# Moving two-input sums and low parts from GpSimd to VectorE in a layer's output mixer and first feed-forward stage, and splitting one weight unit into a spare place

## The chip, the cores and the metric

One Trainium2 chip; the program runs on one of its cores. The engines are TensorE (PE in the profile, with its weight loads as PEld), VectorE (DVE), ScalarE (ACT), GpSimd (POOL) and SyncE (SP, which only issues transfers). The metric is the device time of one execution in microseconds (us): for the kernel before, the median of three runs is 722.89 us (722.44 to 723.54).

## What is computed

One layer of a streaming encoder on a sequence of 512 rows and 1024 columns, all in float32:

```python
u = rms_norm(h, g_mix)
z = u @ w_in                                    # q, k, v of two attentions, two gates
y_a = sliding_window_attention(...) @ w_br_swa
y_b = forgetting_attention(...) @ w_br_fox
mixed = gates[:, :, 0] * y_a + gates[:, :, 1] * y_b
h = h + mixed @ w_mix_out
u = rms_norm(h, g_mlp)
h = h + jnp.square(jax.nn.relu(u @ w_ff1)) @ w_ff2
ple_gate = jax.nn.sigmoid(rms_norm(h, g_ple) @ w_ple_gate)
h = h + ple_gate * (p @ w_ple_proj)             # p: 512 x 256
return rms_norm(h, g_final)
```

## The kernel before

**High and low parts.** Every float32 operand of a matrix product is split into a high part (a rounded copy, made by a cast on ACT, line 332) and a low part (the value minus its high part, a subtraction on two inputs in SBUF, line 334). PE multiplies high by high, high by low and low by high (lines 77 to 79, 918 and 1302). So a block of weights can be used only after its load has landed, ACT has cast it and another engine has subtracted.

**Seven products instead of eight.** The large products (input gates, mixer, both feed-forward stages) are cut into two by two blocks and computed with seven block products, numbered 1 to 7. Their weight operands are quadrants of the weights or sums of quadrants, their other operands are quadrants or sums of quadrants of the activations, and the results are added and subtracted into place. Operand numbers 1, 2 and 3 use a quadrant of the weights as it is; numbers 4 to 7 need a sum. `sum_source` (from line 275) makes that sum in place: by an accumulating transfer from the POOL queue (line 306), by an addition on POOL (line 302: only numbers 6 and 7 of the second column half of the first feed-forward stage) or by an addition on DVE (line 304: numbers 5 and 7 of the second feed-forward stage).

**Units.** The program walks through a list of weight units, of 128x1024 elements in the stages spoken of here. `emit_split(i)` writes the high and low part of unit i into buffers `u<i>h` and `u<i>l`, of which there are four each, used in turn. `advance(i)` splits all units up to i; it is called ahead of each product with the unit that is wanted some steps later, and that distance is what the text calls the look-ahead. After each unit it also issues loads for later units as far as a place for them is free. The names `wq`, `wq_t`, `wq_c` and `wq_gb` are places of raw weights; `emit_dma` (line 271) loads into them from SP. SP runs through its loads in program order, so one that waits for its place holds up all behind it.

**The mixer** (`h + mixed @ w_mix_out`) runs in the order `MIX_STEPS`, "A1 A2 B1 A5 B2 B5 A6 B6 A3 B3 A7 B7 p0 A4 B4 p4": A and B are column halves of the output, the digit is the operand number, and p0 and p4 stand for the product with `w_ple_proj`. Its units are u43 (A1), u44 (A2), u45 (B1), u46 (A5), u47 (B2), u48 (B5), u49 (A6), u50 (B6), u51 (A3), u52 (B3), u53 (A7), u54 (B7), u55 (p0; its halves lie in `at_ff`), u56 (A4), u57 (B4) and u58 (p4, in `at_ff` too). Its other operand is `mixed`, held as `r_a` (upper rows) and `r_b` (lower rows). `branches` adds the two gated attention outputs into them (line 1024 on POOL for `r_a`, line 1030 on DVE for `r_b`), `mix_sum` (line 1064, on POOL) forms the sums of quadrants, and `mix_ops` splits the results into high and low parts, most of the second set into the tile `u_mix`. That tile has 8240 elements a partition; behind a shift of 48 the six operands take 6144, and the last 2048 lie unused. `rows_out` adds each product into the residual `h_sb` (lines 1124 and 1126).

**The first feed-forward stage** comes next: units u59 on, with u62 (b2), u63 (a5), u64 (b5), u65 (a6), u66 (b6) and u67 (a7) ahead of the first units of the second stage, `s2`, which are mixed in from u71 on. Between mixer and stage lies a norm: `norm_scale` gives `n_xn` (line 378), PE transposes it (line 1194), and `t2_top`, `t2_sums`, `t2_sums2`, `t2_sum4` and `t2_rest` form the operands of the stage (lines 1215 to 1245), with their sums `s3` and `s4` on POOL (lines 1235 and 1245). `win_out` adds the products up (line 933), `ff1_lo` and `ff1_act` apply the squared ReLU and split it (line 1430).

**What sets the order.** In the mixer and the first steps of the feed-forward stage the order of ACT's and DVE's instructions is the written one; each engine runs its list in that order, and an instruction that waits holds up all behind it. Low parts listed in `POOL_LO` (units u44, u51 to u54 and u58) are subtracted on POOL, all others on DVE. The places of the raw feed-forward weights are dealt out ahead by a small planner: each block gets the place that comes free first. One of these places, "t2", is planned as free from the unit of ("f1", 1, 2) on, u62, since the tile `p_sb` (the input `p`) lies there before.

Of the kernel before, what the change touches and what calls it, by code (L numbers as in the profile page):

```python
# [8 lines left out]
F32 = mybir.dt.float32  # L9
F32R = mybir.dt.float32r  # L10
AF = mybir.ActivationFunctionType
ALU = mybir.AluOpType
# [35 lines left out]
MIX_STEPS = "A1 A2 B1 A5 B2 B5 A6 B6 A3 B3 A7 B7 p0 A4 B4 p4"  # L48
POOL_LO = [("mx", g, pn) for g, pn in ((0, 2), (0, 3), (1, 3), (0, 7), (1, 7))] + [("pp", 1)]
ET = mybir.EngineType  # L50
# [3 lines left out]
def layer_kernel(ctx: ExitStack, tc: tile.TileContext, x, p, g_mix, w_in, b_forget, swa_sinks,  # L54
# [154 lines left out]
    for n, r in enumerate(used):  # L209
        if first_ff <= r < last_ff:  # L210
            if not free_at:
                for w2 in (True, False):
                    for z, m in enumerate(ring[w2][-2:]):
                        for y in range(2):
                            free_at[w2, z, y] = last_use[used[m]]
                late_places = unit_of["f1", 1, 2]
                free_at.update({"t2": late_places, "c6": late_places,
                                "c7": late_places, "gb": late_places})
# [63 lines left out]
    def sum_source(i):  # L282
# [13 lines left out]
        if pn in (1, 2, 3):  # L296
            q = quadrant(i, pn in (2, 3), pn == 3)
        else:
            q = quadrant(i, 0, pn == 7)
            other = quadrant(i, *{5: (0, 1), 7: (1, 1), 6: (1, 1), 4: (1, 0)}[pn])  # L300
            if key in (("f1", 1, 6), ("f1", 1, 7)):
                nc.gpsimd.tensor_tensor(q, q, other, ALU.add)
            elif key[0] == "s2" and pn in (5, 7):
                nc.vector.tensor_tensor(q, q, other, ALU.add)
            else:
                nc.gpsimd.dma_start(q, other, accum_op=ALU.add)  # L306
        sources[i] = q if key[0] != "f1" and key[0] != "g" else q.rearrange("q k (j c) -> q k j c", c=P)

    def emit_split(i):
# [19 lines left out]
        for a in range(np_):  # L329
            n = shape[1] // np_  # L330
            z = slice(a * n, a * n + n)
            nc.scalar.copy(hi[:, z], src[:, z])  # L332
            on_pool = order[i][0] in POOL_LO
            (nc.gpsimd if on_pool else nc.vector).tensor_tensor(lo[:, z], src[:, z], hi[:, z].bitcast(F32), ALU.subtract)  # L334
        order[i][2] = (hi, lo)
# [667 lines left out]
    def branches(m):  # L1003
# [45 lines left out]
    def mix_place(g, pn):  # L1049
        n = {(0, 1): 0, (0, 2): 1, (0, 4): 4, (0, 5): 2, (0, 6): 3, (0, 7): 6, (0, 3): 7,  # L1050
             (1, 4): 5}.get((g, pn))
        if n is not None:
            return at2.tile([P, 2, 2, 256], F32R, tag=f"d{n}", name=f"mo{g}_{pn}")
        if "u" not in r_whole:
            r_whole["u"] = up.tile([P, 2 * KT * S + SHIFT], F32R, tag="u", bufs=1, name="u_mix")
        n = (1, 2, 5, 6, 3, 7).index(pn) * 1024 + SHIFT
        return r_whole["u"][:, n:n + 1024].rearrange("q (z k s) -> q z k s", z=2, k=2)

    def mix_sum(g, n):
# [3 lines left out]
                       (r11, r22, r11, ALU.add), (r12, r11, r12, ALU.subtract))[n]  # L1063
        nc.gpsimd.tensor_tensor(o, a, b, op)

    look["split"] = 0
    done = None
    for t in P2_STEPS:
# [18 lines left out]
        if t[0] == "br":  # L1087
# [3 lines left out]
            if t[1] == 4:  # L1091
                mix_ops(0, (5, 7, 6, 3))
            if t[1] == 5:
                mix_ops(1, (1,))
# [133 lines left out]
    def t2_sums(tb):  # L1228
# [5 lines left out]
            lambda: nc.vector.tensor_tensor(s1, trs[tb, 1], a21, ALU.subtract))  # L1234
        nc.gpsimd.tensor_tensor(s3, a_raw[0][t2_cols(tb)], a21, ALU.subtract)

# [5 lines left out]

    def t2_sum4(tb):
        a21, s1, s2, s3, s4 = sums[tb]
        nc.gpsimd.tensor_tensor(s4, a_raw[1][t2_cols(tb)], s2, ALU.add)

# [12 lines left out]
    def p_transposed():  # L1259
        pth, ptl = pT[:] = [spare(4 + i, f"pT_{'hl'[i]}", (P, 2, S)) for i in range(2)]  # L1260
        for k in range(2):
            tr = psA.tile([P, 4, P], F32, tag="tr", bufs=3, name=f"p_tr{k}")
            for tb in range(NT):
                nc.tensor.transpose(tr[:, tb, :], p_sb[:, tb, k * P:(k + 1) * P], ident)
            hi_lo(pth[:, k, :].rearrange("q (t c) -> q t c", c=P),
# [57 lines left out]
    for t in MIX_STEPS.split():  # L1323
        if t == "B5":
# [144 lines left out]
    t2_sum4(2)  # L1469
    pp_put(5, pp_mm(5))  # L1470
    advance(f1_0 + 2)
    t2_sums2(3)
    pp_put(6, pp_mm(6))
    pp_put(7, pp_mm(7))
    t2_rest(5)
    advance(f1_0 + 3)
    done, late, later = None, None, {}
    for n, st_ in enumerate(steps):
# [148 lines left out]
```

## Time and profile before

| | |
|---|---|
| median of three runs | 722.89 us (722.44 to 723.54) |
| the profiled execution | 722.85 us |
| its span | 721.1 us |
| mean granted PE clock | 0.995 of full speed |
| PE busy | 702.6 us, 97% of the span |
| DVE busy | 552.3 us, 77% |
| ACT busy | 457.0 us, 63% |
| POOL busy | 130.4 us, 18% |

The mixer's second half and the norm behind it lie at about 311 to 362 us of the span, the first feed-forward stage up to the first product of the second stage at about 362 to 410 us. In the profile a group "engine line op out<-in" is one kind of instruction; "x" counts instructions, and a bracket at the end of a timeline's row names the idle time ahead of an instruction and what ended it. "PEclk" is the share of full speed at which PE was allowed to run.

### The profile page before, as it was taken

To read this page: it belongs to the slowest core of one execution; us is meant where nothing else is said; L and a number is where in the kernel's file an instruction comes from. 1 tells how busy PE (TensorE), PEld (TensorE's weight loads), DVE (VectorE), ACT (ScalarE), POOL (GpSimd) and SP (SyncE) were. 2 spreads that over 40 slices of the span, in tenths; PEclk is the share of its full clock that TensorE was granted. 3 is DMA by queue.
4 is the path that set the end of the run, shared out by engine and by line. 5 is a ranking of instruction groups with operands and counts; after the bars stand their busy time and mean duration, and the time that the engine had idled before them with its cause. 6 is when DMAs were issued, how large, how long until landed. Compare 5 with 4: busy or idle time off the path is not lost.

```text
span 721.1 us, 11513 instructions
## 1 busy us (share of the span) xinstructions
PE 702.6 (97%) x4205; PEld 623.7 (86%) x4205; DVE 552.3 (77%) x918; ACT 457.0 (63%) x851; POOL 130.4 (18%) x152
## 2 busy tenths in 40 slices
PE   8999999999999999989979999999999999999996
PEld 7988888888888998867879889988999889988885
DVE  6557887877696667756897995799669975998555
ACT  6547888779862553345677745875478547875452
POOL 1011211100004501563450102000200011010001
PEclk9999999999999999999999999999999999999998
DMA  9166446660363896498668499947895699268103
GB/s 296 60 171 149 131 111 165 152 178 1 118 205 87 165 331 206 78 225 266 174 156 256 84 270 175 247 115 173 227 241 145 136 259 210 73 142 304 50 2 116
DMA packets 75272, 119.88 MB, mean 166 GB/s; under 512 B 6856, under 2 KB 44752, under 8 KB 75216
## 3 DMA queue, kind: packets, MB, share of 16 engines
q1 hardware_dynamic: 66000, 86.25, 38.1%
q0 software_dynamic: 8928, 32.51, 24.4%
q8 instruction: 33, 0.54, 0.3%
q10 hardware_dynamic: 288, 0.39, 0.2%
q14 instruction: 23, 0.19, 0.1%
HBM read 72.93 MB, written 4.19 MB: 107 GB/s over the span
## 4 chain that ended last, share of the span: by engine, by line
PE 86%; DVE 5%; issue 3%; ACT 3%; DMA 1%; POOL 1%; POOLq 0%; DVEq 0%; ACTq 0%
PE pf L77 5%; PE pf L79 5%; PE pf L78 5%; PE (3, 's2')x L1302 3%; PE (0, 's2')x L1302 3%; PE (2, 's2')x L1302 3%; PE (1, 's2')x L1302 3%; PE h_sc L769 2%; PE h_pv L839 2%; PE h_tr L827 2%; PE psy L77 2%; PE psy L78 2%; PE psy L79 2%; PE vb L483 2%; PE va L483 2%
## 5 line engine op out<-in xcount | busy, mean ns | idle before, releaser
L306 POOL DMA_DIRECT2D wq<-wq x35 | 30.5, 933 | 160.8 <-DVE u43l L334 26.0
L787 ACT ACTIVATE s<-s,h_nm 128x128 f32<-128x128 f32 (+1 forms) x64 | 32.6, 512 | 5.9 <-DVE h_nm L780 5.1
L74 DVE TENSOR_TENSOR h_ptl<-h_tr,h_pth 128x512 fp32r<-128x512 f32 (+2 forms) x40 | 22.9, 604 | 3.9 <-ACT h_pth L73 3.6
L1024 POOL TENSOR_TENSOR r_a<-gl,gl 128x512 f32<-128x512 f32 x4 | 6.1, 1526 | 83.8 <-ACT u25h L332 75.8
L73 ACT CAST h_pth<-h_tr 128x512 fp32r<-128x512 f32 (+2 forms) x40 | 19.5, 523 | 1.8 <-PE h_tr L827 1.4
L368 POOL TENSOR_SCALAR n_ms<-acc 128x1 f32<-128x1 f32 x15 | 4.9, 329 | 83.7 <-ACT sgp L1534 38.9
L483 PE MATMUL va<-wv_h,u 128*128 128x320 f32 x64 | 19.9, 317 | 0.0
L827 PE MATMUL h_tr<-ident,s 128*128 128x128 f32 x136 | 19.6, 277 | 0.2 <-ACT s L807 0.2
L483 PE MATMUL vb<-wv_h,u 128*128 128x328 f32 x64 | 19.6, 313 | 0.0
L1529 DVE TENSOR_TENSOR sgp<-sgp,pp 128x512 f32<-128x512 f32 (+1 forms) x9 | 5.7, 633 | 15.8 <-ACT sgp L1528 15.8
L839 PE MATMUL h_pv<-h_pth,v 128*128 128x256 f32 (+1 forms) x64 | 17.3, 291 | 0.0
L839 PE MATMUL h_pv<-h_ptl,v 128*128 128x256 f32 (+1 forms) x64 | 16.9, 305 | 0.3 <-DVE h_ptl L74 0.3
L1134 ACT ACTIVATE junk<-h_sb 128x512 f32<-128x512 f32 x16 | 10.0, 624 | 11.3 <-DVE h_sb L1124 4.9
L827 PEld LDWEIGHTS h_tr<-ident,s 128*128 128x128 f32 x136 | 15.1, 141 | 2.0 <-ACT s L807 0.6
L807 ACT ACTIVATE s<-s,h_rec 128x128 f32<-128x128 f32 (+2 forms) x32 | 14.2, 483 | 2.4 <-DVE h_rec L801 2.4
L306 POOL DMA_DIRECT2D wq_t<-wq x5 | 4.3, 862 | 62.1 <-DVE u104l L334 25.6
L849 DVE TENSOR_TENSOR h_ao<-h_pv,h_ao 64x512 f32<-64x512 f32 x16 | 10.9, 681 | 6.0 <-ACT h_ao L848 5.8
L1528 ACT ACTIVATE sgp<-psgt,rs 128x512 f32<-128x512 f32 x7 | 4.8, 686 | 14.6 <-PE psgt L79 14.6
L775 DVE CUSTOM_DVE_ANT_0 s<-h_sc,causal 128x128 f32<-128x128 f32 (+3 forms) x32 | 13.8, 483 | 0.3 <-PE h_sc L769 0.3
L801 DVE RECIPROCAL h_rec<-h_den 128x4 f32<-128x4 f32 x16 | 3.0, 185 | 14.5 <-ACT s L787 14.3
L741 POOL TENSOR_SCALAR bswa<-dist 128x256 f32<-128x256 f32 x8 | 7.0, 881 | 37.6 <-DVE h_mx L775 36.5
L74 DVE TENSOR_TENSOR u<-n_tr,u 128x512 fp32r<-128x512 f32 x16 | 10.4, 683 | 4.1 <-ACT u L73 4.1
(1648 smaller groups left out, 2847.6 us busy)
## 6 DMA issues: line engine op xcount, KB each, us to landing
wq<-in_w_ff_dram SPq DMA_DIRECT2D x45, 512.0 KB, 5.8
wq<-wq POOLq DMA_DIRECT2D x35, 512.0 KB, 5.6
wq_c<-in_w_ff_dram SPq DMA_DIRECT2D x9, 512.0 KB, 6.0
wg<-in_w_in_dram SPq DMA_DIRECT2D x4, 1024.0 KB, 5.5
wgw<-in_w_in_dram SPq DMA_DIRECT2D x8, 512.0 KB, 4.8
wgw<-wgw POOLq DMA_DIRECT2D x8, 512.0 KB, 5.7
wq<-in_w_mix_out_dram SPq DMA_DIRECT2D x8, 512.0 KB, 5.1
wpg<-in_w_ple_gate_dram SPq DMA_DIRECT2D x4, 1024.0 KB, 7.6
```

What stands on the lines that cost most here:

```text
L73: nc.scalar.copy(hi, src)
L74: nc.vector.tensor_tensor(lo, src, hi.bitcast(F32), ALU.subtract)
L77: nc.tensor.matmul(ps, lh, rh, start=start, stop=False)
L78: nc.tensor.matmul(ps, lh, rl, start=False, stop=False)
L79: nc.tensor.matmul(ps, ll, rh, start=False, stop=stop)
L306: nc.gpsimd.dma_start(q, other, accum_op=ALU.add)
L483: nc.tensor.matmul(ps, u[:, kk_, ts_], w[:, kk_, c0:c1], start=kk_ == 0 and n == 0, stop=kk_ == KT - 1 and n == 2)
L769: nc.tensor.matmul(ps[:, off:off + n], qs[i][z][:, qb * P:(qb + 1) * P], kk[i][z][:, k0:k0 + n], start=z == 0, stop=z == 1)
L787: nc.scalar.activation(sl, sl, AF.Exp, bias=nm[:, qb:qb + 1], accum_out=den[:, qb:qb + 1])
L827: nc.tensor.transpose(tr[:, n, :], c["s"][:, o, :], ident)
L839: nc.tensor.matmul(pv[:, q0:q0 + nq, :], V2[kb][:, c["v"], :], t[:, o:o + nq, :], start=n == 0, stop=n == 2 * NT - 1, skip_group_check=True)
L1302: nc.tensor.matmul(bank[bkey, bk, i], o, w, start=tg != "" and n == 0, stop=n == 5, skip_group_check=True)
```

## The change

- The low parts of u44, u51 to u54 and u58 are subtracted on DVE; the list `POOL_LO` is gone.
- The sums that fill `r_a` (four of 128x512), the sums of `mix_sum` (eight of 128x512) and the sums `s3` and `s4` of the norm's output (four of 128x512) go from POOL to DVE. `s3` and `s4` are made together, ahead of the fourth and fifth product of the feed-forward stage (index 3 and 4), and the operands 7 and 3 that need them one or two products later than before.
- Of the two weight sums on POOL, that of ("f1", 1, 6) (u66) goes to DVE, and that of ("f1", 1, 7) (u69) becomes an accumulating transfer.
- The high and low part of unit u46 are written into the last 2048 elements of `u_mix`; it takes no buffer of the rings of four.
- The look-ahead in the mixer grows from two units to four at A1, A2 and B1 and to three behind them, from three to four at the last branch product, and may reach u59, the first unit of the feed-forward stage.
- `p_sb` goes from place "t2" into two halves in the pool `tmp`, loaded by two transfers, and "t2" is planned as free from ("mx", 1, 2), u47, on. So the planner deals out other places to later blocks.
- PE's fifth product of `w_ple_proj` goes ahead of the third transposition `t2_pe(2)`, and the splitting of the stage's fourth unit ahead of `t2_rest(5)`.

```diff
-POOL_LO = [("mx", g, pn) for g, pn in ((0, 2), (0, 3), (1, 3), (0, 7), (1, 7))] + [("pp", 1)]
...
-                free_at.update({"t2": late_places, "c6": late_places,
+                free_at.update({"t2": unit_of["mx", 1, 2], "c6": late_places,
...
-            if key in (("f1", 1, 6), ("f1", 1, 7)):
-                nc.gpsimd.tensor_tensor(q, q, other, ALU.add)
-            elif key[0] == "s2" and pn in (5, 7):
+            if key[0] == "s2" and pn in (5, 7) or key == ("f1", 1, 6):
                 nc.vector.tensor_tensor(q, q, other, ALU.add)
             else:
                 nc.gpsimd.dma_start(q, other, accum_op=ALU.add)
...
-            on_pool = order[i][0] in POOL_LO
-            (nc.gpsimd if on_pool else nc.vector).tensor_tensor(lo[:, z], src[:, z], hi[:, z].bitcast(F32), ALU.subtract)
+            nc.vector.tensor_tensor(lo[:, z], src[:, z], hi[:, z].bitcast(F32), ALU.subtract)
...
-            nc.gpsimd.tensor_tensor(r_whole[e][:, j], sig[0], sig[1], ALU.add)
+            nc.vector.tensor_tensor(r_whole[e][:, j], sig[0], sig[1], ALU.add)
...
-        nc.gpsimd.tensor_tensor(o, a, b, op)
+        nc.vector.tensor_tensor(o, a, b, op)
...
-        advance(i + 3)
+        advance(i + 3 if t != ("br", 7) else i + 4)
...
+                early["mx", 0, 5] = [u_mix[:, n:n + 1024].rearrange("q (k c) -> q k c", k=2)
+                                     for n in (6144 + SHIFT, 7168 + SHIFT)]
...
-            p_sb = wk3.tile([P, NT, 256], F32, tag="t2", bufs=1, name="p_sb")
-            nc.sync.dma_start(p_sb, p.rearrange("(t q) c -> q t c", q=P))
+            p_sb = [tmp(f"p_sb{n}", (P, 2, 256)) for n in range(2)]
+            for n in range(2):
+                nc.sync.dma_start(p_sb[n], p[n * 256:n * 256 + 256, :]
+                                  .rearrange("(t q) c -> q t c", q=P))
...
-        advance(min(unit_of[key] + 2, f1_0 - 1))
+        advance(min(unit_of[key] + (4 if t in ("A1", "A2", "B1") else 3), f1_0))
...
-    advance(f1_0)
+    ps = pp_mm(4)
     t2_pe(2)
     t2_sums(2)
-    pp_put(4, pp_mm(4))
+    pp_put(4, ps)
...
-        if n == 1:
-            t2_sum4(3)
-        if n in (3, 5):
-            t2_rest({3: 7, 5: 3}[n])
+        if n in (3, 4):
+            t2_sums34(n - 1)
+        if n in (5, 6):
+            t2_rest({5: 7, 6: 3}[n])
```

The first place at which the order changes is DVE's list in the mixer, from the low part of u46 or u47 on, the units of A5 and B2. `r_b` are quadrants of `mixed`, `u_mix` and `mo_4` operands split from them, `h_sb` the residual. Before (line 334 is the low part, line 74 the operands' low part):

```order
L334 TENSOR_TENSOR u46l<-wq_3191,u46h 128x1024
L74 TENSOR_TENSOR u_mix<-r_b_3444,u_mix 128x512
L74 TENSOR_TENSOR mo_4_3486<-r_b_3446,mo_4_3486 128x512
L334 TENSOR_TENSOR u47l<-wq_3321,u47h 128x1024
L1124 TENSOR_TENSOR h_sb<-mxx_3500,h_sb 128x512
L1124 TENSOR_TENSOR h_sb<-mxx_3507,h_sb 128x512
L74 TENSOR_TENSOR u_mix<-r_b_3446,u_mix 128x512
L334 TENSOR_TENSOR u48l<-wq_3258,u48h 128x1024
```

After, at the same place (lines 330, 73, 1058 and 1122 are lines 334, 74, 1064 and 1124 of before):

```order
L330 TENSOR_TENSOR u47l<-wq_3321,u47h 128x1024
L73 TENSOR_TENSOR u_mix<-r_b_3444,u_mix 128x512
L73 TENSOR_TENSOR mo_4_3490<-r_b_3446,mo_4_3490 128x512
L1058 TENSOR_TENSOR r_b_3446<-r_b_3446,r_b_3353 128x512
L1058 TENSOR_TENSOR r_b_3353<-r_b_3351,r_b_3353 128x512
L330 TENSOR_TENSOR u48l<-wq_3258,u48h 128x1024
L1058 TENSOR_TENSOR r_b_3351<-r_b_3446,r_b_3351 128x512
L1058 TENSOR_TENSOR r_b_3444<-r_b_3351,r_b_3444 128x512
L330 TENSOR_TENSOR u49l<-wq_3191,u49h 128x1024
L1122 TENSOR_TENSOR h_sb<-mxx_3508,h_sb 128x512
```

The four sums of `mix_sum` now stand in DVE's list, and the low parts u47l, u48l and u49l come ahead of the first sums into `h_sb`, where only u46l and u47l came before.

The second place is DVE's list in the first feed-forward stage. `u_('f1', …)` are sums of products, `o_0_1` and `o_1_1` squared results, `at_ff` operands of the stage, `u_a`, `u_s_2` and `u_s_3` sums of the norm's output. Before:

```order
L334 TENSOR_TENSOR u64l<-wq_3414,u64h 128x1024
L1218 TENSOR_TENSOR at_ff<-u_s_2_3923,at_ff 128x4x128
L1218 TENSOR_TENSOR at_ff<-u_s_3_3963,at_ff 128x4x128
L933 TENSOR_TENSOR u_('f1', 1)_4070<-('f1', 1)y,u_('f1', 1)_4070 128x512
L1430 TENSOR_TENSOR o_0_1_4116<-u_('f1', 0)_4042,o_0_1_4116 128x512
L1215 SCALAR_TENSOR_TENSOR at_ff<-u_s_3_3964,at_ff 128x4x128
L334 TENSOR_TENSOR u65l<-wq_3321,u65h 128x1024
L334 TENSOR_TENSOR u66l<-wq_3414,u66h 128x1024
```

After (line 301 is the weight sum of u66, lines 1242 and 1243 are `s3` and `s4`):

```order
L330 TENSOR_TENSOR u64l<-wq_3321,u64h 128x1024
L929 TENSOR_TENSOR u_('f1', 1)_4066<-('f1', 1)y,u_('f1', 1)_4066 128x512
L301 TENSOR_TENSOR wq_3321<-wq_3321 128x1024
L1242 TENSOR_TENSOR u_s_2_3932<-u_a_3494,u_a_2_3929 128x512
L1430 TENSOR_TENSOR o_0_1_4110<-u_('f1', 0)_4039,o_0_1_4110 128x512
L1243 TENSOR_TENSOR u_s_2_3933<-u_a_3495,u_s_2_3931 128x512
L330 TENSOR_TENSOR u65l<-wq_3414,u65h 128x1024
L1242 TENSOR_TENSOR u_s_3_3963<-u_a_3494,u_a_3_3960 128x512
L1430 TENSOR_TENSOR o_1_1_4151<-u_('f1', 1)_4066,o_1_1_4151 128x512
L1243 TENSOR_TENSOR u_s_3_3964<-u_a_3495,u_s_3_3962 128x512
L330 TENSOR_TENSOR u66l<-wq_3321,u66h 128x1024
```

Between u64l and u65l stood five instructions and stand five, of which three (the lines 301, 1242 and 1243) stood on POOL before; between u65l and u66l stood none and stand three.

The third place is SP's list of transfers. Before:

```order
L1331 DMA p_sb<-in_p_dram 128x4x256
L271 DMA wq_3191<-in_w_ff_dram 128x4x256
L271 DMA wq_3414<-in_w_ple_proj_dram 128x2x512
L271 DMA wq_3414<-in_w_ff_dram 128x4x256
L271 DMA wq_3258<-in_w_ple_proj_dram 128x2x512
```

After:

```order
L270 DMA wq_3191<-in_w_ff_dram 128x4x256
L1330 DMA p_sb_3607<-in_p_dram 128x2x256
L1330 DMA p_sb_3608<-in_p_dram 128x2x256
L270 DMA wq_t_3622<-in_w_ple_proj_dram 128x2x512
L270 DMA wq_3321<-in_w_ff_dram 128x4x256
L270 DMA wq_3414<-in_w_ff_dram 128x4x256 x2
L270 DMA wq_3258<-in_w_ple_proj_dram 128x2x512
```

The load of `p` now stands behind a load of feed-forward weights into the place `wq_3191`, and the first half of `w_ple_proj` goes to place "t2" (`wq_t`) instead of one that a mixer unit frees.

More of the change, by code (lines that the diff above doesn't have):

```diff
@@ L1053, in mix_place @@
             return at2.tile([P, 2, 2, 256], F32R, tag=f"d{n}", name=f"mo{g}_{pn}")
-        if "u" not in r_whole:
-            r_whole["u"] = up.tile([P, 2 * KT * S + SHIFT], F32R, tag="u", bufs=1, name="u_mix")
         n = (1, 2, 5, 6, 3, 7).index(pn) * 1024 + SHIFT
@@ L1092, in layer_kernel @@
                 mix_ops(0, (5, 7, 6, 3))
+                u_mix = up.tile([P, 2 * KT * S + SHIFT], F32R, tag="u", bufs=1, name="u_mix")
+                r_whole["u"] = u_mix
+                early["mx", 0, 5] = [u_mix[:, n:n + 1024].rearrange("q (k c) -> q k c", k=2)
+                                     for n in (6144 + SHIFT, 7168 + SHIFT)]
             if t[1] == 5:
@@ L1234, in t2_sums @@
             lambda: nc.vector.tensor_tensor(s1, trs[tb, 1], a21, ALU.subtract))
-        nc.gpsimd.tensor_tensor(s3, a_raw[0][t2_cols(tb)], a21, ALU.subtract)
     def t2_sums2(tb):
@@ L1241, in t2_sums2, with t2_sums34 @@
         put(6, tb, s2)
-    def t2_sum4(tb):
+    def t2_sums34(tb):
         a21, s1, s2, s3, s4 = sums[tb]
-        nc.gpsimd.tensor_tensor(s4, a_raw[1][t2_cols(tb)], s2, ALU.add)
+        nc.vector.tensor_tensor(s3, a_raw[0][t2_cols(tb)], a21, ALU.subtract)
+        nc.vector.tensor_tensor(s4, a_raw[1][t2_cols(tb)], s2, ALU.add)
     def t2_rest(pn):
@@ L1263, in p_transposed @@
             for tb in range(NT):
-                nc.tensor.transpose(tr[:, tb, :], p_sb[:, tb, k * P:(k + 1) * P], ident)
+                nc.tensor.transpose(tr[:, tb, :], p_sb[tb // 2][:, tb % 2, k * P:(k + 1) * P], ident)
             hi_lo(pth[:, k, :].rearrange("q (t c) -> q t c", c=P),
@@ L1468, in layer_kernel @@
     t2_sums(3)
-    t2_sum4(2)
     pp_put(5, pp_mm(5))
@@ L1474, in layer_kernel @@
     pp_put(7, pp_mm(7))
+    advance(f1_0 + 3)
     t2_rest(5)
-    advance(f1_0 + 3)
     done, late, later = None, None, {}
```

## The prediction

> **What bounds the kernel now.** I read the page first, then PE's waits, then the two stretches of the program that the change touches.
>
> ```profile
> span 721.1 us, 11513 instructions
> PE 702.6 (97%) x4205; PEld 623.7 (86%) x4205; DVE 552.3 (77%) x918; ACT 457.0 (63%) x851; POOL 130.4 (18%) x152
> ```
>
> PE is busy for 97% of the span. Only what makes PE wait, or run at less than its clock, can change the time; 721.1 − 702.6 = 18.5 us stand idle in all, with head and tail. The change gives PE no work and takes none from it. So I look for the waits of PE, by the instruction that ended them (in total, times, longest, in us):
>
> ```profile
> PE ('f1', 0)x L918 <- DVE u65l L334: 3.1, 1, 3.1
> ...
> PE n_tr L1194 <- DVE n_xn L378: 1.2, 1, 1.2
> PE mxx L1302 <- DVE u50l L334: 0.8, 1, 0.8
> PE ('f1', 1)y L918 <- DVE u62l L334: 0.8, 1, 0.8
> PE n_tr L1194 <- DVE u L1218: 0.7, 1, 0.7
> ...
> PE mxz L1302 <- POOL u51l L334: 0.5, 1, 0.5
> PE mxx L1302 <- ACT u50h L332: 0.5, 1, 0.5
> PE ('f1', 1)y L918 <- ACT u62h L332: 0.5, 1, 0.5
> PE mxx L1302 <- DVE h_sb L1126: 0.4, 1, 0.4
> PE pspp L78 <- DVE at_ff L334: 0.3, 1, 0.3
> ```
>
> Ten rows lie in the part that the change touches. Seven belong to the mixer and the norm (u50h 0.5, u50l 0.8, u51l 0.5, at_ff 0.3, h_sb 0.4, u 0.7, n_xn 1.2), in sum 4.4 us; three to the first feed-forward stage (u62h 0.5, u62l 0.8, u65l 3.1), in sum 4.4 us too. Busy times by stretch (us, then PE, PEld, DVE, ACT, POOL with counts, PEclk, DMA share, GB/s), ahead of them a slice of the gate stage:
>
> ```profile
> 220.00:240.00 20.00, 20.00 (x123) 18.01 (x122) 14.72 (x13) 7.89 (x10) 9.00 (x9) 1.00 0.46 87
> ...
> 311.00:361.90 50.90, 46.08 (x250) 37.64 (x248) 34.96 (x46) 31.26 (x59) 24.13 (x20) 1.00 0.81 232
> 361.90:410.20 48.30, 44.31 (x315) 41.89 (x316) 43.60 (x48) 36.05 (x53) 10.55 (x8) 0.96 0.67 170
> ```
>
> In the mixer PE loses 50.90 − 46.08 = 4.8 us while DVE has 16 us to spare: it is chains that make PE late, not an engine that is full. In the feed-forward stretch DVE is busy for 43.6 of 48.3 us, and the clock is at 0.96.
>
> **The clock.** The 3.1 us wait has a second price, which the chain of waits shows behind it (start, us, engine, count):
>
> ```profile
> 374.88 3.98 PE ('f1', 0)x L918 x22
> 378.86 3.21 PE ('f1', 1)x L918 x24
> 382.07 2.83 PE ('f1', 0)x L918 x24
> ```
>
> A product of 24 matmuls takes 2.83 us, so 22 should take 2.83 × 22 / 24 = 2.59 and took 3.98; the next took 3.21. That is 1.39 + 0.38 = 1.8 us at a lower clock, which agrees with 0.04 × 48.3 = 1.9 of the stretch. With waits and clock gone, PE alone would need 48.3 − 4.4 − 1.8 = 42.1 us there.
>
> [...]
>
> **The mixer: why its chains are late.** DVE's and POOL's timelines there (start, us, engine, line, operation):
>
> ```profile
> 301.97 2.39 DVE L74 TENSOR_TENSOR u_mix<-r_b,u_mix 128x512 fp32r<-128x512 f32 x1
> 304.29 2.32 DVE L334 TENSOR_TENSOR u48l<-wq,u48h 128x1024 fp32r<-128x1024 f32 x1
> 306.52 0.68 DVE L74 TENSOR_TENSOR u_mix<-r_b,u_mix 128x512 fp32r<-128x512 f32 x1
> 307.73 1.21 DVE L334 TENSOR_TENSOR u49l<-wq,u49h 128x1024 fp32r<-128x1024 f32 x1
> 332.31 1.40 DVE L378 SCALAR_TENSOR_TENSOR n_xn<-h_sb,n_rs,g_mlp_bc 128x512 f32<-128x512 f32 x2
> 335.28 3.58 DVE L378 SCALAR_TENSOR_TENSOR n_xn<-h_sb,n_rs,g_mlp_bc 128x512 f32<-128x512 f32 x2
> ```
>
> ```profile
> 301.87 3.65 POOL L1064 TENSOR_TENSOR r_b<-r_b,r_b 128x512 f32<-128x512 f32 x2
> 306.90 1.77 POOL L306 DMA_DIRECT2D wq<-wq  x2 [1.38 <-DVE u48l L334]
> 314.85 2.71 POOL L334 TENSOR_TENSOR u51l<-wq,u51h 128x1024 fp32r<-128x1024 f32 x1
> 335.61 2.71 POOL L334 TENSOR_TENSOR at_ff<-wq,at_ff 128x1024 fp32r<-128x1024 f32 x1 [8.09 <-ACT at_ff L332]
> ```
>
> While POOL adds (301.87 to 305.52), an operation on DVE with two inputs in SBUF takes 2.39 where its like takes 0.68, and u48l takes 2.32 where u49l takes 1.21. The same pairing shows in the norm: n_xn takes 3.58 under the subtraction on POOL, 1.40 without, and PE's wait of 1.2 hangs on it. The excess of 1.7 + 1.1 + 2.2 = 5.0 us is time in which DVE waits for POOL; the new list takes away both partners.
>
> [...]
>
> The delay does not stay on DVE. POOL's accumulating transfer of 306.90 waits for u48l, and its data lands only 4.71 us later; u50h is cast right behind, and PE waits for u50h and u50l:
>
> ```profile
> 306.90 4.71 DMA wq<-wq
> ```
>
> ```profile
> 311.69 1.05 ACT L332 CAST u50h<-wq 128x1024 fp32r<-128x1024 f32 x1
> ```
>
> After the change nothing is ahead of this chain on POOL but transfers, u48l loses its 1.1 us and the 1.7 ahead of it, and the units are split up to two earlier, since u46 takes no buffer of the rings. The four sums put into DVE's list there cost 4 × 0.68 = 2.7 us, about the 2.8 that the stretches gave back; but the look-ahead puts the chain one to two products ahead, 2.8 to 5.7 us by the row of 24 matmuls, against 0.5 + 0.8 of wait. u51l is done in 1.21 instead of 2.71 and its buffers are earlier too. The wait for h_sb goes with the mixer's sums behind u50, and pspp (0.3) with the earlier split. For n_xn DVE pays 1.2 for the low part of u58 and is spared 2.2; PE also has the fifth product of `w_ple_proj`, about 1.4 us by half a product of 24, put ahead of the transpositions that waited 0.7 and 1.2. I take 4.1 of the 4.4 as gone: 0.3 stays, for the first of the transpositions. The least would be 2.0, if only u50, u51 and pspp went (0.5 + 0.8 + 0.5 + 0.3 = 2.1), the most 4.4.
>
> The sums of `r_a` and the first four of `mix_sum` lie in the gate stage: 8 × 0.68 = 5.4 us on a DVE that is busy for 14.72 of 20 while PE is at 20.00. They cost nothing; without that cover they would cost at most their 5.4.
>
> **The feed-forward stretch.** Here the change takes stretches from DVE and gives it work.
>
> ```profile
> 366.79 3.50 DVE L1218 TENSOR_TENSOR at_ff<-u_s,at_ff 128x512 fp32r<-128x512 f32 x2
> 370.81 2.28 DVE L1430 TENSOR_TENSOR o<-u_('f1', 0)_4042,o 128x512 fp32r<-128x512 f32 x1
> 373.62 1.21 DVE L334 TENSOR_TENSOR u65l<-wq,u65h 128x1024 fp32r<-128x1024 f32 x1
> ```
>
> ```profile
> 365.44 1.76 POOL L306 DMA_DIRECT2D wq<-wq  x2 [4.54 <-DVE u63l L334]
> 366.96 2.78 POOL L302 TENSOR_TENSOR wq<-wq 128x1024 f32<-128x1024 f32 x1
> 369.70 2.84 POOL L302 TENSOR_TENSOR wq<-wq,wq 128x1024 f32<-128x1024 f32 x1
> ```
>
> Under the two additions on POOL, two of DVE's operations took 3.50 where two take 1.4, and one 2.28 where one takes 0.68: 2.1 + 1.6 = 3.7 us of stretch go. Four sums and one addition come: 4 × 0.68 + 1.2 = 3.9. So DVE needs 43.6 − 3.7 + 3.9 = 43.8 us, while PE needs 42.1. **DVE becomes what bounds the stretch**, by 1.7 us if it never idles, and it will idle a little.
>
> The wait for u65l is a chain: u63l's end frees the transfer that adds u65's quadrants (POOL's row of 365.44 waited for it), about 4.7 us to its landing by the row of 306.90, then 1.05 of cast and 1.21 of low part, about 7 us, with the issue 7.2. PE has the products of u63 and u64 in that time, 2 × 2.83 = 5.7. So 1.5 to 1.6 of the 3.1 stay, the rest was the two additions that DVE and POOL stood in. u62's 1.3 shrinks to about 0.5, since u62 to u64 are split one step earlier. New are about 0.5 for u66 and u67, behind the three rows that now stand between u65l and u66l, and about 1.3 for the low parts and sums that run into the first products of the second stage, behind which DVE is full. In sum 0.5 + 1.6 + 0.5 + 1.3 = 3.9 of wait against 4.4 before. The clock's 1.8 should go: the longest wait would be 1.6, and the waits for u50h and u50l, 1.3 together, left the mixer's clock at 1.00. By these the stretch takes 42.1 + 3.9 = 46.0, a gain of 2.3; some 0.4 is lost behind it, where DVE still catches up. From below the stretch can't be shorter than 43.8, a gain of 4.5; from above, a wait that stays at 3.1 keeps the 1.8, and with the new 1.8 of waits and no u62 gain the stretch would take about 50.1, 1.8 longer than now.
>
> The transfer that takes the place of the addition for u69 costs POOL 0.9 (half of 1.77) instead of 2.84; it lands some 5 us later, with four products (11 us) before its use: nothing.
>
> **The sum.** Against the profiled execution, 722.85 (span 721.1, 1.75 around it; the median is 722.89, the same): 722.85 − 4.1 − 2.3 + 0.4 = 716.85, which I give as **717.0 us**, since the new places of raw weights may cost a little that no row shows.
>
> **The rivals.**
>
> *DVE's load is worse than that.* With DVE at 43.8 against 42.1, one more product late, or a wait for u65 near 3 us, brings the clock's 1.8 back: 717.0 + 1.8 + 0.7 = 719.5. For it speaks that DVE's new rows stand right ahead of u65l and u66l. Against it speaks that the two weight additions on POOL, which stretched DVE by 3.7, are gone. Chance 0.18.
>
> *All waits go.* If the earlier splits cover u65's chain and DVE is never late, the whole 8.8 of waits and the 1.8 go: 722.85 − 10.6 = 712.2. Against it is DVE's 43.8 in a stretch that would then have 42.1. Chance 0.07.
>
> *No gain.* If DVE and POOL had merely taken turns, DVE would now do itself what it waited for. For the mixer, 4 sums and 6 low parts cost it 4 × 0.68 + 6 × 1.21 = 10.0 against 5.0 of stretch, and if chains run over DVE, its 5.0 of new load eats the 4.1, with the stage's 1.9 lost to DVE being full: 722.9. Against it: DVE is idle for 16 of the mixer's 50.9 us. Chance 0.06. [...]
>
> *Slower: `p` lands late.* SP's timeline and SP's waits:
>
> ```profile
> 317.84 0.37 SPq L271 DMA_DIRECT2D wq<-in_w_ff_dram  x1
> ```
>
> ```profile
> SPq L271 <- DMA wq<-wq: 7.8, 1, 7.8
> ```
>
> A load of 512 KB in the chain of waits, and PE's use of `p`:
>
> ```profile
> 322.28 5.44 DMA wq<-in_w_ple_proj_dram
> ```
>
> ```profile
> 320.25 1.03 PE L1264 MATMUL p_tr<-ident,p_sb 128*128 128x128 f32 x8
> ```
>
> Before, the load of `p` stood ahead of the feed-forward block that waited for 7.8 us and went out at 317.84; now it stands behind it. If that block went out no earlier, `p` would land near 317.84 + 5.44 = 323.3, and PE wants it at 320.25 less the 1.8 that it is earlier there, 318.4: a wait of 4.9, with the clock's 1.8 behind it, 717.0 + 6.7 = 723.7. It decides if the accumulating transfer that frees the place lands later than about 313. I expect it to land at 310 to 312, since the unit is split one or two products (2.8 to 5.7 us) earlier. Chance 0.06.
>
> **How the numbers follow.** The forecast gets 0.63, with 714 to 719 as its own range (the bounds: 4.4 and 4.5 gained below, less for each that both at once are unlikely; 2.1 in the mixer with 1.9 behind it above). Left out of 714.0 to 720.5 are the cases of 712.2, 722.9 and 723.7, with 0.07 + 0.06 + 0.06 = 0.19. A measurement of this kernel can tell 0.2%, 1.4 us, from no change: faster means below 721.4. That holds for the forecast and the first two rivals, 0.63 + 0.18 + 0.07 = 0.88; same 0.06; slower 0.06.
>
> **What would show it.** In the profile after: POOL without a subtraction or sum of 128x512 or 128x1024, DVE's like operations at 0.68 and 1.21 throughout; no waits for u50, u51 and n_xn; a wait for u65l of 1 to 2 us and no clock below 1.00 behind it; DVE at over 0.93 of the feed-forward stretch. The forecast is wrong if PE waits for `p_tr` or u65l by 3 us, if DVE's operations stay stretched without POOL (then the cause was not POOL), or if new waits of over a us stand in the rows of u66 to u77.

## The result, and the profile after

The changed kernel takes 717.25 us (median of four runs, 716.11 to 719.32), the one before beside it 722.66 us (722.25 to 723.54): a ratio of 0.9927, with an interval of 0.9899 to 0.9954. In a second set of six runs it took 716.7 us, with a ratio of 0.9913 (0.9897 to 0.9929). The forecast was 717.0. The profiled execution below is the one of 719.32 us, the longest.

The page after:

```profile
span 717.6 us, 11507 instructions
PE 702.9 (98%) x4205; PEld 622.3 (87%) x4205; DVE 550.5 (77%) x941; ACT 456.6 (64%) x851; POOL 87.8 (12%) x129
```

POOL does 42.6 us less, yet DVE is busy for no longer than before (550.5 against 552.3): the 23 operations that it took over cost about what its stretched ones had cost. PE's waits after:

```profile
PE (0, 's2')z L1300 <- DVE u81l L330: 1.0, 1, 1.0
PE ('f1', 0)x L914 <- DVE u65l L330: 0.8, 1, 0.8
PE psgt L77 <- DVE u173l L321: 0.7, 2, 0.4
...
PE (0, 's2')z L1300 <- DVE u77l L330: 0.5, 1, 0.5
PE ('f1', 0)x L914 <- ACT u65h L329: 0.4, 1, 0.4
```

All seven waits of the mixer and the norm are gone. u65's 3.1 became 0.8 + 0.4, and the longest that were not there before stand at u77, u81 and u173 (a unit of `w_ple_gate`). To see where the time went I cut both executions at the same instructions: the mixer's first matmul, the feed-forward stage's first, the first of its second quarter (`('f1', 2)x`), the first of the per-layer gate (`psgt`) and the last. Busy times by stretch as in the prediction, before:

```profile
293.00:353.10 60.10, 55.65 (x257) 44.25 (x256) 42.98 (x53) 32.55 (x58) 30.26 (x26) 1.00 0.75 201
353.10:436.90 83.80, 79.44 (x505) 72.19 (x504) 74.46 (x86) 55.98 (x79) 18.77 (x16) 0.98 0.73 190
436.90:667.80 230.90, 230.90 (x1528) 210.92 (x1527) 192.41 (x229) 153.81 (x212) 31.23 (x38) 1.00 0.75 188
667.80:714.00 46.20, 46.20 (x235) 39.06 (x233) 26.05 (x42) 20.48 (x43) 4.27 (x10) 1.00 0.10 36
```

and after:

```profile
293.90:347.90 54.00, 54.00 (x257) 44.76 (x257) 43.97 (x62) 32.12 (x58) 10.72 (x16) 1.00 0.86 228
347.90:429.60 81.70, 78.72 (x505) 70.24 (x504) 72.97 (x91) 55.26 (x78) 9.50 (x11) 1.00 0.76 199
429.60:662.60 233.00, 232.12 (x1529) 211.53 (x1528) 189.08 (x223) 151.25 (x207) 31.22 (x38) 1.00 0.75 189
662.60:710.50 47.90, 47.07 (x235) 38.74 (x233) 29.39 (x48) 22.56 (x47) 4.90 (x10) 1.00 0.06 23
```

The mixer gained 6.1 us and PE is busy in all of it. The feed-forward stage's first quarter gained 2.1. Then 2.1 are lost in the long middle and 1.7 at the end. The middle's loss is this execution's own, as the second profile of the same kernel shows below; of the end's, 1.1 are in both profiles.

### The profile page after: what moved, and what is told of

It is laid out like the page before. It is cut to its first block, busy times and chain, and to the rows that moved or that the text cites. A ratio compares the mean times of both kernels' runs of the same rounds, so it can differ in the third digit from the quotient of the medians.

```text
span 717.6 us, 11507 instructions
## 1 busy us (share of the span) xinstructions
PE 702.9 (98%) x4205; PEld 622.3 (87%) x4205; DVE 550.5 (77%) x941; ACT 456.6 (64%) x851; POOL 87.8 (12%) x129
## 4 chain that ended last, share of the span: by engine, by line
PE 64%; DVE 13%; DMA 9%; issue 8%; ACT 5%; SPq 1%; POOL 0%; POOLq 0%; ACTq 0%; DVEq 0%
DMA wq<-wq 5%; PE pf L76 5%; PE pf L78 5%; PE pf L77 5%; PE mxx L1300 3%; PE h_sc L765 3%; PE (1, 's2')x L1300 2%; PE h_pv L835 2%; PE h_tr L823 2%; PE psy L76 2%; PE psy L77 2%; PE psy L78 2%; PE vb L479 2%; PE va L479 2%; PE ('g', 1, 2)x L914 2%
## 5 line engine op out<-in xcount | busy, mean ns | idle before, releaser
L303 POOL DMA_DIRECT2D wgw<-wgw x8 | 7.1, 971 | 101.7 <-DVE u25l L330 77.7
L835 PEld LDWEIGHTS h_pv<-h_ptl,v 128*128 128x128 f32 x64 | 12.1, 188 | 1.7 <-DVE h_ptl L73 0.8
L771 DVE CUSTOM_DVE_ANT_0 s<-h_sc,bswa 128x256 f32<-128x256 f32 (+1 forms) x32 | 10.7, 384 | 3.1 <-PE h_sc L765 3.1
```

The lines of the kernel that those rows point to most:

```text
L771: nc.vector.tensor_tensor_reduce(out=s[:, o:o + n], in0=ps[:, off:off + n], in1=c["bias"](qb), scale=1.0, scalar=NEG, op0=ALU.add, op1=ALU ...
L835: nc.tensor.matmul(pv[:, q0:q0 + nq, :], V2[kb][:, c["v"], :], t[:, o:o + nq, :], start=n == 0, stop=n == 2 * NT - 1, skip_group_check=True)
```

## The experiments

Theories at the start: **both halves** (mine: the quiet POOL and the earlier splits each take away their waits), **engines alone**, and **schedule alone** (look-ahead, places and the unit in `u_mix`).

**The changed kernel again** (e1), with no edit.

> The changed kernel once more, to learn its spread and to have a second profile. My theory: the mixer has no wait left, and what differs between executions (716.1 to 719.3 so far) lies behind the feed-forward stretch, where DVE is full and the weight sums of the second stage (u80, u81) come late. Then a median of 716.5 to 718, and a profile of a faster execution has less than the 5.5 us of loss behind 412 us. Rival: the spread is in the start of the kernel or in the mixer; then the profiles differ ahead of 350 us.

716.7 us. Its profile, of a 716.13 us execution, agrees with the first to 0.1 us in the mixer and in the first quarter, and differs in the middle and at the end:

```profile
429.10:660.00 230.90, 230.90 (x1528) 211.00 (x1527) 189.57 (x224) 152.24 (x208) 31.14 (x38) 1.00 0.76 191
660.00:707.30 47.30, 46.78 (x235) 38.86 (x233) 28.77 (x47) 21.95 (x46) 4.88 (x10) 1.00 0.06 23
```

So of the 3.2 us between these two executions 2.7 lie behind 429 us, and 0.1 in the parts that the forecast summed. What causes it there stays open: the waits for u77 and u81, which I had suspected, are the same in both (0.5, and 0.9 to 1.0). The end is 1.1 us longer than before in this short execution too, so that loss belongs to the change.

**Only the engines** (e2): the kernel before with these lines alone.

```diff
-            on_pool = order[i][0] in POOL_LO
-            (nc.gpsimd if on_pool else nc.vector).tensor_tensor(lo[:, z], ...)
+            nc.vector.tensor_tensor(lo[:, z], ...)
...
-        nc.gpsimd.tensor_tensor(o, a, b, op)
+        nc.vector.tensor_tensor(o, a, b, op)
```

(and so for `r_a`, `s3`, `s4` and u66's weight sum; u69's becomes a transfer).

> The kernel before with only the engines changed: low parts, sums of r_a, of the mixer and of the norm's output on DVE, u66's weight sum on DVE and u69's as a transfer; look-ahead, places and the unit in u_mix stay as before. My theory (both halves count): the stretches go and with them the waits for u50, u51 and n_xn, about 2.5 to 3.5 us, and 1 to 3 us in the feed-forward stretch: 717.5 to 720. Rival that the earlier splits and places do it alone: 722 to 723.5. Rival that the engines do it alone: 716.5 to 717.5, as the changed kernel.

717.1 us (716.78 to 718.13), ratio 0.9919 (0.9901 to 0.9938). My theory, 717.5 to 720, fell here: by the whole time the engines alone give as much as the whole change. PE's waits, then busy times by stretch (the two stages, and 8 us within the mixer):

```profile
PE pspp L77 <- ACT at_ff L330: 1.3, 1, 1.3
...
PE pspp L78 <- DVE at_ff L331: 0.8, 1, 0.8
```

```profile
293.20:351.80 58.60, 56.31 (x258) 45.55 (x257) 45.82 (x64) 33.27 (x59) 10.42 (x16) 0.97 0.78 206
351.80:430.80 79.00, 77.46 (x505) 70.30 (x504) 72.59 (x90) 55.63 (x78) 9.49 (x11) 1.00 0.80 207
...
326.00:334.00 8.00, 5.94 (x18) 4.12 (x17) 5.19 (x7) 4.61 (x8) 0.00 (x0) 0.79 0.77 259
```

The mixer gains only 1.5: PE now waits for the first half of `w_ple_proj`, 1.3 and 0.8. ACT casts that half at 327.31, as late as before the change (327.74); in e1, with the earlier place, it does so at 319.87. Behind the waits the granted clock is 0.50 from 330.0 to 333.4 us, which makes 0.79 of the 8 us. But the first quarter then takes 79.0, where the whole change has 81.7. Together the two stages take 143.9 before, 137.6 here, 135.7 with the whole change. So the schedule is worth 1.9 more in these stages; at the end it loses 1.1 to 1.8, since the last stage takes 46.1 here, 47.2 in e3 and 47.3 to 47.9 with both halves.

**Only the schedule** (e3): the changed kernel with all that back on POOL.

> The changed kernel with every moved operation back on POOL (the low parts of six units, all sums, the two weight sums); the longer look-ahead, the places and the unit in u_mix stay. My theory: 719 to 721.5, since DVE is stretched again and u65 waits for two additions on POOL with the clock's 1.8 behind it. Rival that the earlier splits and places do it alone: 716.5 to 718. Rival that the engines do it alone: 722 to 723.5.

722.93 us, ratio 1.0007 (0.9992 to 1.0022): of the whole time's gain nothing is left, less than my 719 to 721.5. The waits for u50 and u51 are gone here too, but others stand in their place (PE's waits, DVE's timeline, POOL's timeline, in three fences):

```profile
PE ('f1', 0)x L918 <- DVE u65l L334: 4.3, 1, 4.3
PE n_tr L1196 <- DVE u L1220: 1.8, 1, 1.8
```

```profile
334.16 1.41 DVE L378 SCALAR_TENSOR_TENSOR n_xn<-h_sb,n_rs,g_mlp_bc 128x512 f32<-128x512 f32 x2 [3.93 <-POOL n_rs L371]
...
363.95 5.97 DVE L1434 TENSOR_TENSOR o<-u_('f1', 0)_4039,o 128x512 fp32r<-128x512 f32 x1 [0.29 <-ACT o L1412]
```

```profile
330.69 2.39 POOL L334 TENSOR_TENSOR at_ff<-wq,at_ff 128x1024 fp32r<-128x1024 f32 x1 [5.86 <-ACT at_ff L332]
333.18 0.30 POOL L368 TENSOR_SCALAR n_ms<-acc 128x1 f32<-128x1 f32 x1
333.57 0.56 POOL L371 TENSOR_TENSOR n_rs<-n_ms,mhalf 128x1 f32<-128x1 f32 x1
```

The norm is no longer stretched (1.41). It is queued: the two small operations that give `n_rs` stand behind the subtraction on POOL, which itself waits 5.86 us for its cast and then takes 2.39, and DVE waits 3.93 for them. The earlier split moved the subtraction ahead of them. In the feed-forward stage an operation that takes 0.68 alone is held for 5.97 us, through the two weight sums and the sum behind them on POOL (363.15 to 369.36), and u65l comes after it. Mixer and first quarter take 57.0 + 85.4 = 142.4.

**One piece back on POOL at a time**, the changed kernel each time: the six low parts (e4), the sums of `r_a` and the mixer (e5), the two weight sums (e6), `s3` and `s4` (e12). For example e6:

```diff
-            if key[0] == "s2" and pn in (5, 7) or key == ("f1", 1, 6):
+            if key in (("f1", 1, 6), ("f1", 1, 7)):
+                nc.gpsimd.tensor_tensor(q, q, other, ALU.add)
+            elif key[0] == "s2" and pn in (5, 7):
```

> The changed kernel with only the low parts of u44, u51 to u54 and u58 back on POOL. My theory: n_xn is stretched again by the subtraction of u58 if it still falls beside it (1.2 us), u51 to u54 are covered by the longer look-ahead: 717.5 to 719. If the low parts were the heart of the gain: 720 to 722. If they don't count: 716.5 to 717.5.

> The changed kernel with only the sums of r_a and of the mixer (lines 1024 and 1064 of before) back on POOL. Theory after the first four runs: in the mixer either half is enough, the earlier splits or the quiet POOL, since both kernels with one half alone lost their waits for u50 and u51. Then 716.3 to 717.5, with u48l stretched again and no wait behind it. Rival, as the prediction had it: the stretch of u48l costs its wait for u50 again, 718 to 719.

> The changed kernel with only the two weight sums of u66 and u69 back on POOL. Theory: they are what u65 waits for; a wait of 2.5 to 4 us for u65l comes back with the clock's loss behind it, and part of it is given back at u77 and u81, where DVE then is not late: 718.5 to 720.5. Rival that the norm's sums s3 and s4 or the low parts on POOL made u65 late: 716.3 to 717.5.

> The changed kernel with only the sums s3 and s4 of the norm's output back on POOL, at their new places. Theory: the two weight sums on POOL were what made u65 late, not these: 716.3 to 717.5, with DVE's operations beside them stretched to 1.3 to 2.4 us. Rival that every two-input sum on POOL in this stretch makes u65 late by its own length: a wait for u65l of 2.5 us or more and 718.5 to 721.

Against 716.7: e4 718.93 (+2.2), e5 717.24 (+0.5, inside the spread of these runs), e6 721.46 (+4.8, more than I expected), e12 718.01 (+1.3). They come to more than e3's 6.2. A part of it is that what is lost ahead is saved behind: in e3 and e6 PE waits neither for u77 nor for u81. The rest was not traced. e4's size was as I expected, its cause was not: n_xn takes 1.42 and waits 3.94 for `n_rs`, as in e3, and the mixer takes 56.4 instead of 54.0. e5 is what the theory of that time said: u48l is stretched again (2.34), and with the units split earlier no wait of PE comes of it. In e6 (PE's waits, POOL, DVE, and the stretch around it):

```profile
PE ('f1', 0)x L916 <- DVE u65l L332: 3.1, 1, 3.1
```

```profile
360.65 2.78 POOL L301 TENSOR_TENSOR wq<-wq 128x1024 f32<-128x1024 f32 x1
363.40 2.81 POOL L301 TENSOR_TENSOR wq<-wq,wq 128x1024 f32<-128x1024 f32 x1
```

```profile
361.69 2.29 DVE L1245 TENSOR_TENSOR u_s<-u_a,u_s 128x512 f32<-128x512 f32 x1
363.91 2.85 DVE L1432 TENSOR_TENSOR o<-u_('f1', 0)_4039,o 128x512 fp32r<-128x512 f32 x1
...
367.29 1.21 DVE L332 TENSOR_TENSOR u65l<-wq,u65h 128x1024 fp32r<-128x1024 f32 x1
```

```profile
364.00:376.00 12.00, 8.34 (x50) 7.94 (x49) 11.16 (x12) 9.00 (x13) 3.93 (x3) 0.72 0.77 182
```

The two additions on POOL hold up two of DVE's operations by 1.6 and 2.2 us, u65l comes at 367.29 instead of 364.98 (its row stands below), and the granted clock is 0.50 from 366.9 to 373.7 us, 0.72 over these 12. The first quarter takes 84.0 instead of 81.6. This profile is of e6's fastest execution, 718.25; its others took 720.1 to 723.6, so half of the 4.8 is seen here and the other half was not. In e12 the sums on POOL do the same on a smaller scale (first quarter 82.9); my range there (716.3 to 717.5) was too low:

```profile
361.03 3.10 DVE L301 TENSOR_TENSOR wq<-wq 128x1024 f32<-128x1024 f32 x1
...
367.50 3.04 DVE L330 TENSOR_TENSOR u66l<-wq,u66h 128x1024 fp32r<-128x1024 f32 x1
```

Both of these operations take 1.22 with POOL quiet.

**The loss at the end: places dealt in another order** (e7). The late places go into the planner's list first, and of each ring the second place.

```diff
-                for w2 in (True, False):
-                    for z, m in enumerate(ring[w2][-2:]):
-                        for y in range(2):
-                            free_at[w2, z, y] = last_use[used[m]]
                 late_places = unit_of["f1", 1, 2]
                 free_at.update({"t2": unit_of["mx", 1, 2], "c6": late_places,
                                 "c7": late_places, "gb": late_places})
+                for w2 in (True, False):
+                    for z, m in reversed(list(enumerate(ring[w2][-2:]))):
+                        for y in range(2):
+                            free_at[w2, z, y] = last_use[used[m]]
```

> The changed kernel with the places of the raw feed-forward weights dealt in another order, so that the first block of w_ple_gate gets a place that comes free some units earlier, as it had before the change. Theory: the 1.2 to 1.7 us that PE loses at the start of the per-layer embedding in the changed kernel come from that place, and go: 714.8 to 716, against 716.7. Rival that they come from elsewhere (norm, DVE): 716.3 to 717.2. If the other places disturb the feed-forward stages: over 717.2.

715.2 us (714.62 to 717.49), ratio 0.9902 (0.9885 to 0.9919). By the whole time this can't be told from the changed kernel, whose interval overlaps; the stage shows it. When the loads of `w_ple_gate` go out, in the changed kernel and then in e7 (SP's timeline, a fence each), and e7's last stage by the busy times:

```profile
649.40 3.12 SPq L270 DMA_DIRECT2D wpg<-in_w_ple_gate_dram  x3
```

```profile
615.88 0.37 SPq L270 DMA_DIRECT2D wpg<-in_w_ple_gate_dram  x1
...
646.05 4.24 SPq L270 DMA_DIRECT2D wpg<-in_w_ple_gate_dram  x3
```

```profile
659.90:706.10 46.20, 46.20 (x235) 39.04 (x233) 26.73 (x44) 20.89 (x44) 5.18 (x10) 1.00 0.06 24
```

In the changed kernel the first load goes out with two more, 13 us ahead of `psgt` (662.6); in e7 it went out alone, 44 us ahead of it, and the last stage takes 46.2 again, as before the change. In the kernel before it had gone out alone at 651.85, 16 us ahead. So the order in which places are dealt out around 310 us decided a load 300 us later. That it is the early "t2" that shifted it was not tested alone.

**DVE's load in the first quarter** (e8, e9, e10, e11). The condition that picks a weight sum for DVE is widened or narrowed:

```diff
# e8, on the changed kernel: four sums of the second stage's first quarter as transfers
-            if key[0] == "s2" and pn in (5, 7) or key == ("f1", 1, 6):
+            if key[0] == "s2" and key[1] > 1 and pn in (5, 7) or key == ("f1", 1, 6):
# e9, on e7: u80's sum on DVE (e10: u65's, ("f1", 0, 6); e11: both)
+            if key[0] == "s2" and pn in (5, 7) or key in (("f1", 1, 6), ("s2", 1, 6)):
```

> The changed kernel with the four weight sums 5 and 7 of the first quarter of the second feed-forward stage as accumulating transfers instead of additions on DVE (4 x 1.2 us less on DVE between 385 and 410 us). Theory that DVE's load makes u77 and u81 late: the 2.2 us lost at 400 to 416 us shrink to about 1 or less: 715 to 716.3. Rival that u80's accumulating transfer is the cause: no gain or a loss, since more transfers are queued, 716.5 to 719.

> The kernel with the places dealt anew, and in it the weight sum of u80 (product 6 of the second column half, second feed-forward stage, first quarter) as an addition on DVE instead of an accumulating transfer. Theory: the chain u77l, transfer (5.2 us), u80h, u80l is what makes u80 and u81 late, and an addition of 1.2 us shortens it by 4 us: of the 2.2 us lost at 400 to 416 us about 1.2 go: 713.7 to 714.8, against 715.2. Rival that DVE is simply full there: 1.2 us more on it make it 715.2 to 716.5.

> The kernel with the places dealt anew, and in it the weight sum of u65 as an addition on DVE instead of an accumulating transfer. Theory: the transfer is the long link of the chain that PE waits for at u65 (0.8 for the low part, 0.4 to 0.6 for the high part), and the wait goes. If DVE bounds the stretch up to 416 us, as the prediction has it, PE then only waits longer at u77 and u81, and the end stays: 714.8 to 715.8. Rival that PE keeps what it gains there: 713.5 to 714.5.

> Both weight sums, u65's and u80's, as additions on DVE, on the places dealt anew. If each removes its own chain and DVE has room: 712.5 to 714, the fastest. If DVE bounds the stretch: 714.8 to 716.5, no better than the places alone (715.2).

e8 took 724.32 us, ratio 1.0025 (1.0013 to 1.0038), above both ranges that I had set: DVE has four sums of 1.22 us less to do and the kernel is no faster than before the change. PE's waits, the chain of waits and the stretch behind:

```profile
PE (0, 's2')x L1300 <- ACT u82h L329: 3.3, 1, 3.3
...
PE (0, 's2')z L1300 <- DVE u77l L330: 0.8, 1, 0.8
```

```profile
410.23 0.54 POOL wq_c L303
410.77 7.41 DMA wq_gb<-wq
...
418.26 1.05 ACT u82h L329
```

```profile
415.00:430.00 15.00, 11.28 (x37) 8.42 (x36) 8.12 (x10) 6.10 (x6) 0.00 (x0) 0.77 0.97 250
```

u77's wait grew, and u82 waits for an accumulating transfer that takes 7.41 us, the second of three issued within 1.1 us: an addition of 1.2 us on DVE was replaced by 7 us in a chain. Behind the wait the granted clock is 0.50 from 418.8 to 425.6 us, 0.77 over the 15 of the stretch. The wait of 3.3 and half of these 6.8 make 6.7 of the 7.6 us that e8 is slower than the changed kernel. e9 is the counter-test, 714.08 us (713.72 to 714.54), ratio 0.9882 (0.9865 to 0.9898): the transfer of u80 in the changed kernel (chain of waits) and its low part there (DVE's timeline), then the addition in the transfer's place in e9 (DVE's timeline):

```profile
401.20 5.16 DMA wq_c<-wq
406.38 1.06 ACT u80h L329
```

```profile
407.46 1.23 DVE L330 TENSOR_TENSOR u80l<-wq_c,u80h 128x1024 fp32r<-128x1024 f32 x1 [2.12 <-ACT u80h L329]
```

```profile
400.20 1.22 DVE L301 TENSOR_TENSOR wq_c<-wq_c,wq 128x1024 f32<-128x1024 f32 x1
...
405.40 1.22 DVE L330 TENSOR_TENSOR u80l<-wq_c,u80h 128x1024 fp32r<-128x1024 f32 x1
```

Counted from each execution's first matmul of the stage (347.93 and 347.00), u80l comes 1.1 us earlier. u81's wait is gone, DVE's hole ahead of u80l (2.12 us idle) is filled, and the first quarter takes 80.5 where e7 has 81.6. e10 and e11 did not do the same for u65: 715.27 and 714.63 us, against 715.2 and 714.08 without (714.63 lies between the two ranges that I had set for e11). In e10 and, without the edit, in e1 (DVE's timeline):

```profile
358.45 1.23 DVE L301 TENSOR_TENSOR wq<-wq,wq 128x1024 f32<-128x1024 f32 x1
...
364.87 1.22 DVE L330 TENSOR_TENSOR u65l<-wq,u65h 128x1024 fp32r<-128x1024 f32 x1
```

```profile
364.98 1.23 DVE L330 TENSOR_TENSOR u65l<-wq,u65h 128x1024 fp32r<-128x1024 f32 x1 [0.83 <-ACT u65h L329]
```

The sum is done at 359.7, while in e1 the transfer had landed when u65h was cast at 363.9; yet u65l starts no earlier, 364.87 against 364.98 with the mixer's start at 293.0 and 293.5: in e10 DVE works through its list from 357.2 without a hole. In e1 its hole ahead of u65l is 0.83 us, shorter than the addition of 1.22, and from u65l on it has none until the one ahead of u80l: between 365 and 400 us it is busy for 35.00 us. There DVE is the bound, as forecast; at u80 the transfer was.

e9 is the fastest kernel of the study, 8.5 us under the one before (722.58 beside it).

## Why the prediction was right, point by point

**The time and its sign** were right, 717.0 against 717.25 and 716.7. That it came this close is in part luck: the mixer gave 2.0 more than summed, and the end of the kernel took 1.1 to 1.7 that the sum did not have.

**The mixer: the direction right, 4.1 us mis-sized, measured 6.1.** I summed the waits as the profile lists them. PE loses more with each, as its timeline before shows:

```profile
311.67 0.61 PE L1302 MATMUL mxx<-u49h,mo 128*128 128x512 f32 x2
312.78 0.50 PE L1302 MATMUL mxx<-u50h,u_mix 128*128 128x512 f32 x1 [0.50 <-ACT u50h L332]
314.04 0.50 PE L1302 MATMUL mxx<-u50l,u_mix 128*128 128x512 f32 x1 [0.76 <-DVE u50l L334]
```

Matmuls of this kind start 0.23 us apart there and last 0.39, overlapping (the rows ahead of these, at 310.99, 311.22 and 311.44). The wait counts from the end of the last one. From 312.78 to 314.04 PE lost 1.26 − 0.23 = 1.03, listed as 0.76; by the same reckoning the wait ahead of it cost 0.65, listed as 0.50. In the stage 60.10 − 55.65 = 4.45 were idle, and 55.65 − 54.00 = 1.65 counted as busy. Seven waits of 0.15 to 0.27 more than listed would make 1.1 to 1.9; that is an estimate from these two.

**What took the mixer's waits away.** The stretch of DVE by POOL, the first reason given, was real, and u48l's 2.32 is 1.22 after. But it was not needed: e3 and e5 keep the sums on POOL and show no wait for u50. Nor were the earlier splits: e2 has none of them and no such wait. Either is enough. Each half by itself pays elsewhere: without the earlier place for `w_ple_proj` 2.1 us of wait and 3.4 us at a clock of 0.50 (e2), with the low part of u58 on POOL 1.8 us of PE's wait behind the queue ahead of `n_rs` (e3). The second of these is a price that the prediction did not see; it took the norm's wait for a stretch only.

**The feed-forward stretch** came out nearly as summed: 2.1 us gained in the first quarter against 2.3 less 0.4. Between the prediction's own ends (from PE's wait for u62 to the third matmul of u77) the 48.3 us became 45.1, forecast 46.0, with DVE busy for 43.15 of them, 0.96, forecast over 0.93; about 1 us of that is lost again behind. u65's wait is 0.8 + 0.4 to 0.6, forecast 1.6; the clock stayed at 1.00. u62 and u66 wait for nothing, so 1.0 of the forecast waits did not come; instead the second stage's first products lost 2.1 (u77, u81 and h_sb, listed as 1.7), where 1.3 + 0.4 was set. That DVE would be the bound is shown from u65 to u79 by its list without a hole in e1, and by e10. e2's shorter first quarter, which PE entered later, fits it, though its sums `s3` and `s4` stand at their old places. For the stretch as a whole it was too strong: u81's wait was a transfer's, and e9 gives DVE 1.22 us more and is 1.1 faster there.

**The largest single piece** of the change by these runs are the two weight sums (e6, 4.8 us by the medians). The chain of u65 and its clock, as the prediction had it, account for the 2.4 that the profile shows; the rest stays open.

**The term that was missing**: the new places of raw weights. "May cost a little that no row shows" was set at 0.15 and turned out as 1.1 us at the end of the kernel (1.7 in the longest execution), and e7 takes it away.

**The sums in the gate stage** cost nothing that shows: the mixer's first matmul comes at 293.0 us before the change and between 292.9 and 294.0 in the kernels that have these sums on DVE.

**The rivals.** DVE's load did not bring the clock's loss back: u65 waited 1.2 to 1.4 us and the clock stayed at 1.00 there. Nor did all waits go: those at u65, u77 and u81 are left. `p` did not land late: the block load in front of it went out at 310.70 in e1, 7.1 us earlier than before, and nothing waits for `p_tr`. The rival of no gain from moving work between POOL and DVE is refuted by e2. The pairing that the prediction had read from DVE's and POOL's timelines held in every stretch seen: operations on DVE that take 0.68 or 1.22 alone took 0.91 (before, at 360.53 us) to 5.97 (e3, at 363.95 us) beside two-input operations of 128x512 or 128x1024 on POOL, in e6 and e12 again (1.78 to 3.10), and in the profile after, where POOL has none of these, none was stretched. The 5.97 of e3 lies beside three operations of POOL.

## What to carry to other kernels

POOL's few two-input operations cost DVE here about as much time as doing them itself: it took 23 of them over and was busy no longer (550.5 us against 552.3). So count DVE's stretched operations, and what is queued on POOL behind each long one, POOL's own waits included. Replace a transfer by an addition where a chain waits for the transfer, and leave it where the other engine is full anyway; which of the two holds was seen here from the hole (idle time) of that engine ahead of the late row. At u80 it was longer than the addition (2.12 against 1.22 us) and the kernel gained; at u65 it was shorter (0.83) and nothing was gained. And when a planner deals out places, look at the last stage that it serves as well as at the one that was edited.

## What was not expected of the hardware

- The clock was lost without a single long wait: after waits of 1.30 and 0.76 us within 2.6 us the granted clock was 0.50 for the next 3.4 us (e2). In the kernel before, 0.50 and 0.76 within 1.8 us left it at 1.00, and so did a single wait of 1.8 us (e3, 1.00 over the mixer); with one of 1.6 us (e10) the mean clock of the execution was 0.997, as in the changed kernel. In these traces the loss came as a stretch of 3.4 us at 0.50 (before, 376.2 to 379.6 us; e2, 0.79 over 8 us; e12, 0.86 over 12) or of about 6.8 us (e6, 0.72 over 12 us; e8, 0.77 over 15; e3, 0.96 over the 85.4 of the first quarter).
- At the two waits worked out above, PE lost 0.15 and 0.27 us more than the profile lists: the matmuls ahead of them last 0.39 and 0.50, and without a wait the next starts 0.23 after their start.
- An accumulating transfer of 512 KB that took 5.16 us issued alone (the changed kernel, 401.20) took 7.41 as the second of three issued within 1.1 us (e8).
- An operation on DVE that takes 0.68 us alone took 5.97 beside three operations on POOL, one after the other (e3, 363.15 to 369.36 us).
